# Splitting part of the mixing weights ahead of time, during the FFNs, and fetching the two parts from DRAM

## The chip, the core and the metric

The kernel runs on one core of a Trainium2 chip. The metric is the device time of one execution in microseconds. Engines are named as in the profile: PE (TensorE, matmuls), PEld (its weight loads), DVE (VectorE), ACT (ScalarE), POOL (GpSimd), SP (SyncE, which issues every DMA of this kernel, in one queue).

## What is computed

Two layers of a hybrid backbone over 256 context and 256 latent tokens of width 1024. Each layer is an FFN half step, a token mixing and a second FFN half step:

```
for l in range(2):
    x = ffn_sublayer(x, ...); s = ffn_sublayer(s, ...)          # swiglu, 1024 -> 2*2816 -> 1024
    hx, hs = modulate(rms_norm(x)), modulate(rms_norm(s))
    out_x, out_s = token_mixing(hx, hs, ...)                    # one input projection mix_w_in, then
                                                                # retention + attention + RWKV-7,
                                                                # three branch projections, gates, w_out
    x = x + gate * out_x;  x = ffn_sublayer(x, ...)
    if l == 0: s = s + gate * out_s;  s = ffn_sublayer(s, ...)
```

Everything is float32. The shift, scale and gate vectors ("ada") come from a conditioning vector times a 1024 x 9216 matrix per layer.

## The kernel before

**Dense products.** A float32 product is made of three passes on PE: both operands are split into a high part (rounded to the PE's fp32r format) and the remainder, and `mm3` (lines 185 to 188) adds high x high, high x low and low x high. Activations lie feature-major, 512 tokens as columns: 256 of the context, 256 of the latent stream. In layer 1, after the mixing's inputs, only the 256 latent columns are left.

**Weights.** All weights of a stage lie in DRAM in the order of use, in groups of four 128 x 128 blocks (128 x 512 float32, 256 KB): `w0a`, `w0b`, `w0c` are the first FFN, the mixing and the second FFN of layer 0, `w1a`, `w1b`, `w1c` those of layer 1. Each FFN has 132 groups; `w0b` is loaded in 214 and `w1b` in 211 group loads (a few groups are loaded twice). `Weights.get` brings a group in:

```
raw = s.mk([128, PB * 128], "raw", 8)[:, :cols]
hi = s.mk([128, PB * 128], "whi", 4, F32R)[:, :cols]
lo = s.mk([128, PB * 128], "wlo", 3, F32R)[:, :cols]
s.last = nc.sync.dma_start(out=raw, in_=...).ins        # L113, SP
nc.scalar.copy(hi, raw)                                  # L114, ACT
nc.vector.tensor_sub(lo, raw, hi.bitcast(F32))           # L115, DVE
```

The last argument of a tile is the number of its buffers: 8 raw tiles, 4 high parts, 3 low parts. A raw buffer comes free when DVE has made the low part of it, a `whi` or `wlo` buffer when PE has used it.

**Stages.** In time the program runs: first FFN of layer 0 (up to about 385 us), first mixing (to about 1270), second FFN of layer 0 (to about 1655), first FFN of layer 1 (to about 2047), second mixing (to about 2737), last FFN. Beside the FFNs run the ada tasks: `ada_tile` (lines 227 to 243) loads a 512 KB tile `m` on SP (L234, 3 buffers) and reduces it with two DVE instructions (L236, L237). In the first FFN some ada tiles go through PE instead (`adaT`, L254). The mixing holds the recurrences: `rw_prep`, `rw_merge`, `rw_chain` (lines 901 to 1112) are chains of small steps that go back and forth between PE, ACT, DVE, and POOL, where 31 pairs of POOL instructions (L1006, L1007) invert small triangular blocks, with DMAs through DRAM on both sides.

**Order.** The order on each engine is not the order of the code: a list scheduler with its own model of times places the instructions of all engines while the program is built, so loads of a later stage can stand ahead of work of an earlier one. On the chip every engine, and the SP queue too, then works strictly in the order that was written; an instruction that waits holds up all behind it. `tc.issue_after(mark)` keeps a DMA behind another one.

Of the kernel before, what the change touches and what calls it, by code (L numbers as in the profile page):

```python
# [7 lines left out]
F32 = mybir.dt.float32  # L8
F32R = mybir.dt.float32r
# [16 lines left out]
PB = 4  # L26
# [60 lines left out]


class Weights:
    def __init__(s, nc, mk, ap, plan, pool=False):  # L90
        s.pool = pool
        s.nc, s.mk, s.ap, s.plan = nc, mk, ap, plan
        s.n = sum(len(b) for _, b in plan)
        s.at, s.pos, s.cur = 0, 0, {}

# [8 lines left out]
    def get(s, t, n=1):  # L104
        p = t // PB
        if p not in s.cur:
            nc = s.nc
            cols = min(PB, s.n - p * PB) * 128
            raw = s.mk([128, PB * 128], "raw", 8)[:, :cols]
            hi = s.mk([128, PB * 128], "whi", 4, F32R)[:, :cols]  # L110
            lo = s.mk([128, PB * 128], "wlo", 3, F32R)[:, :cols]
            o = p * PB * 16384
            s.last = nc.sync.dma_start(out=raw, in_=s.ap[o:o + 128 * cols].rearrange("(p c) -> p c", p=128)).ins  # L113
            nc.scalar.copy(hi, raw)  # L114
            nc.vector.tensor_sub(lo, raw, hi.bitcast(F32))  # L115
            s.cur = {q: v for q, v in s.cur.items() if q == p - 1}
            s.cur[p] = (hi, lo)
        hi, lo = s.cur[p]
        c = (t % PB) * 128
        return hi[:, c:c + 128 * n], lo[:, c:c + 128 * n]  # L120


def body(nc, tc, I, O, es, dbg=None):
# [251 lines left out]
    def ffn(l, base, W, H, S, tasks, last=False, lead=True):  # L375
        c = span(S)
        gate = sm(16, "gate", 2).rearrange("p (k s) -> p k s", s=2)
        slots, done = 2 * FT + 16 - 8, [0, 0]

        def run(n):  # L380
            done[0] += n
            while done[1] < min(len(tasks), len(tasks) * done[0] // slots):
                tasks[done[1]]()
                done[1] += 1

        for hf in range(2):
            hid = []
            if hf == 0:
                os = [ps(t) for t in ("mm", "mm", "rx", "rx", "ap", "sc")[:2 * G3]]
                first(W, "first", H, [c] * len(os), os, 1 if lead and len(S) == 2 else 0)  # L390
            for j in range(HF):
                p = hf * HF + j
                if p < G3:
                    pg, pu = os[2 * p:2 * p + 2]
                else:
                    pg, pu = ps("mm"), ps("mm")
                    dense(W, f"g{p}", H, c, pg)
                    dense(W, f"u{p}", H, c, pu)
                sg = ft()
                A.activation(sg[:, c], pg[:, c], AF.Silu)  # L400
                V.tensor_tensor(sg[:, c], sg[:, c], pu[:, c], ALU.mult)  # L401
                h = pair("hid", HF)
                split(hl(h, c), sg[:, c])
                hid.append(h)
                run(2)
            if hf == 0:
                V.tensor_scalar(gate, mods[l, base + 2], 0.5, None, ALU.mult)
            for n in range(KT):
                if hf == 1 and n == KT - 1 and len(S) == 2:
                    last_out(W, f"o{hf}.{n}", hid, gate)  # L410
                    run(1)
                    continue
                po = ps("mm")
                dense(W, f"o{hf}.{n}", hid, c, po)
                residual(n, po, gate, S)
                run(1)
                if hf == 1:
                    if last:
                        SP.dma_start(out=O["out"][n], in_=xs[n][:, CS[1]])
                    else:  # L420
                        sq_acc(n, S)

    def load_x():
        for kt in range(KT):
# [797 lines left out]
    ada_cols()  # L1222
    ada_cond()
    vf = dp.tile([4, 128, 512], F32, name="vf", tag="vf")
    for l in range(2):
        S = both if l == 0 else lat

        def tasks(ll, ms, mark=None):
            return [lambda m=m, kt=kt: ada_tile(ll, m, kt, False, mark) for m in ms for kt in range(KT)]

        if l == 0:
            def fine(kt):
                ada_pe(0, 1, kt)
                ada_tile(0, 0, kt, True)
            H = norm(0, 0, 0, both, fine)
            tk = tasks(0, range(2, 9))
        else:
            H = norm(1, 0, 0, both)
            ada_cond()
            tk = tasks(1, range(5, 9))  # L1240
        W = Weights(nc, mk, I[f"w{l}a"], plan_ffn("f1i", "f1o"))
        ffn(l, 0, W, H, both, tk, lead=(l > 0))
        if not RC:
# [3 lines left out]
        xd = dp.tile([8, 128, 512], F32, name="xd", tag="xd", bufs=2)  # L1247
        for kt in range(KT):
            mark = SP.dma_start(out=xd[kt], in_=xs[kt]).ins
        W = Weights(nc, mk, I[f"w{l}b"], plan_mix(l), True)  # L1250
        ms, mark = mix(l, W, H, S, vf, mark, mst)
        mix_out(l, W, ms, S, xd)
        H = norm(l, 2, 6, S)
        tk = []
        if l == 0:
            with tc.issue_after(mark):
                ada_cond()
            tk = tasks(1, range(5), mark)
        W = Weights(nc, mk, I[f"w{l}c"], plan_ffn("f2i", "f2o"))
        ffn(l, 6, W, H, S, tk, last=(l == 1))  # L1260

# [103 lines left out]
```

## Time and profile before

| | |
|---|---|
| three runs | 2952.3, 2956.5, 2960.07 us (median 2956.5) |
| the profiled execution | 2952.92 us, of it 2951.1 us span |
| granted PE clock, mean of the span | 0.963 |
| busy: PE, PEld, DVE, ACT, POOL | 95%, 81%, 68%, 45%, 13% |
| DMA | 400.97 MB, 136 GB/s on average |

The span is the time from the first to the last instruction of the trace; 1.8 us lie outside it. Busy time says what an engine did, not what the others waited for. A busy PE is not a PE at its peak: matmuls overlap in the pipeline, and the clock granted to it may be lower than full. In the views below "waited for" rows read: engine, line and what it waits for; the time in total, how often, and the longest. SPq is SP's queue.

### The profile page before, as it was taken

Reading aid. Unit: us, or ns where it says so; the run is one execution under the profiler, and the core shown is the slowest. Engines: PE = TensorE matmul, PEld = TensorE weight load, DVE = VectorE, ACT = ScalarE, POOL = GpSimd, SP = SyncE. Lnnn points to the kernel's source line nnn. Section 1 sums busy time; section 2 is a strip of 40 time slices with the busy share of each in tenths; the row PEclk is TensorE's granted clock in tenths of the full one; section 3 lists DMA queues with packets and bytes.
Section 4 is the critical chain, followed back from the end, with each engine's and each line's share of the span. In section 5 each row is a group of like instructions: output and inputs, shape, how many; then the busy total and the mean of one; then the engine's idle time right before and its main releaser. Section 6 shows DMA issues by size and latency. Waiting matters only on the chain.

```text
span 2951.1 us, 47422 instructions
## 1 busy us (share of the span) xinstructions
PE 2796.3 (95%) x16761; PEld 2387.8 (81%) x16761; DVE 1999.8 (68%) x4677; ACT 1320.8 (45%) x2968; POOL 375.0 (13%) x1068
## 2 busy tenths in 40 slices
PE   8999999889999999899999999999989898999999
PEld 7888888677877787688888888888878787888999
DVE  7967668666685766467746567455787776577655
ACT  3322245556555654333223332223467665564544
POOL 0000000522032211000000000000033433330000
PEclk9999999889999999999999999999999999799999
DMA  7656444212332146433534435353334233146554
GB/s 268 232 188 192 155 127 132 76 49 82 115 97 78 50 128 216 154 104 126 184 136 162 145 121 173 108 174 120 123 109 112 80 114 113 53 131 202 171 179 154
DMA packets 259727, 400.97 MB, mean 136 GB/s; under 512 B 78752, under 2 KB 96288, under 8 KB 259488
## 3 DMA queue, kind: packets, MB, share of 16 engines
q1 hardware_dynamic: 259488, 397.93, 42.5%
q8 instruction: 132, 2.16, 0.3%
q14 instruction: 107, 0.88, 0.1%
HBM read 368.33 MB, written 25.82 MB: 134 GB/s over the span
## 4 chain that ended last, share of the span: by engine, by line
PE 79%; DVE 6%; POOL 5%; DMA 4%; ACT 2%; issue 2%; SPq 1%; POOLq 0%; DVEq 0%; ACTq 0%
PE ps_mm L186 20%; PE ps_mm L188 20%; PE ps_mm L187 20%; POOL cst L1007 3%; POOL cst L1006 2%; PE ps_mm L364 2%; PE ps_po L774 1%; PE ps_rf L974 1%; DVE wlo L115 1%; PE ps_rx L1084 1%; DMA z<-td 1%; PE ps_po L559 1%; PE ps_rx L1077 1%; PE ps_rx L364 1%; PE ps_rx L1105 1%
## 5 line engine op out<-in xcount | busy, mean ns | idle before, releaser
L114 ACT CAST whi<-raw 128x512 fp32r<-128x512 f32 x954 | 564.6, 617 | 698.9 <-PE ps_mm L187 362.4
L186 PE MATMUL ps_mm<-hall,whi 128*128 128x512 f32 (+1 forms) x2320 | 841.6, 363 | 5.7 <-DVE ft L693 1.5
L188 PE MATMUL ps_mm<-hall,wlo 128*128 128x512 f32 (+1 forms) x2320 | 841.1, 363 | 2.3 <-DVE wlo L115 2.2
L187 PE MATMUL ps_mm<-hall,whi 128*128 128x512 f32 (+1 forms) x2320 | 838.3, 362 | 0.0
L115 DVE TENSOR_TENSOR wlo<-raw,whi 128x512 fp32r<-128x512 f32 x954 | 645.5, 692 | 98.2 <-ACT whi L114 68.4
L186 PEld LDWEIGHTS ps_mm<-hall,whi 128*128 128x128 f32 x2320 | 440.8, 190 | 75.2 <-ACT kv L711 2.0
L188 PEld LDWEIGHTS ps_mm<-hall,wlo 128*128 128x128 f32 x2320 | 439.0, 189 | 75.9 <-DVE wlo L115 4.7
L187 PEld LDWEIGHTS ps_mm<-hall,whi 128*128 128x128 f32 x2320 | 439.7, 190 | 71.3 <-issue 0.3
L186 PE MATMUL ps_mm<-hid,whi 128*128 128x512 f32 (+1 forms) x737 | 260.7, 354 | 0.0
L187 PE MATMUL ps_mm<-hid,whi 128*128 128x512 f32 (+1 forms) x737 | 259.9, 354 | 0.0
L188 PE MATMUL ps_mm<-hid,wlo 128*128 128x512 f32 (+1 forms) x737 | 257.4, 354 | 0.0
L1006 POOL TENSOR_TENSOR cst<-acc,cst 128x60 f32<-128x60 f32 (+24 forms) x496 | 167.9, 339 | 613.7 <-DMA acc<-ad__10934 59.4
L373 DVE SCALAR_TENSOR_TENSOR x<-ps_mm,cst,x 128x256 f32<-128x256 f32 x136 | 61.0, 481 | 193.7 <-PE ps_mm L188 193.6
L401 DVE TENSOR_TENSOR ft<-ft,ps_mm 128x512 f32<-128x512 f32 (+1 forms) x80 | 49.6, 621 | 209.0 <-PE ps_mm L188 199.4
L851 POOL TENSOR_TENSOR ll<-lora,lh 128x512 fp32r<-128x512 f32 x8 | 10.5, 1316 | 1367.9 <-DMA cst<-gup 953.9
L1007 POOL TENSOR_TENSOR cst<-cst 128x60 f32<-128x60 f32 (+24 forms) x496 | 177.2, 357 | 38.0
L236 DVE SCALAR_TENSOR_TENSOR ft<-m,cd 128x1024 bf16<-128x1024 f32 x136 | 163.0, 1221 | 8.7 <-DMA m<-ada 8.7
L237 DVE SCALAR_TENSOR_TENSOR m<-m,cd 128x1024 f32<-128x1024 f32 x136 | 165.6, 1223 | 0.7
L187 PEld LDWEIGHTS ps_mm<-hid,whi 128*128 128x128 f32 x737 | 139.1, 189 | 19.5
L186 PEld LDWEIGHTS ps_mm<-hid,whi 128*128 128x128 f32 x737 | 139.0, 189 | 19.4
L188 PEld LDWEIGHTS ps_mm<-hid,wlo 128*128 128x128 f32 x737 | 138.5, 189 | 19.5
L186 PE MATMUL ps_mm<-whi,hall 128*128 128x256 f32 x416 | 120.7, 291 | 8.2 <-DVE rr_v L799 5.1
(339 smaller groups left out, 4518.7 us busy)
## 6 DMA issues: line engine op xcount, KB each, us to landing
m<-ada SPq DMA_DIRECT2D x136, 512.0 KB, 4.3
raw<-w0b SPq DMA_DIRECT2D x214, 256.0 KB, 2.9
raw<-w1b SPq DMA_DIRECT2D x211, 256.0 KB, 3.1
raw<-w0a SPq DMA_DIRECT2D x132, 256.0 KB, 2.8
raw<-w0c SPq DMA_DIRECT2D x132, 256.0 KB, 4.4
raw<-w1a SPq DMA_DIRECT2D x132, 256.0 KB, 4.3
raw<-w1c SPq DMA_DIRECT2D x132, 256.0 KB, 3.9
gd<-ft SPq DMA_DIRECT2D x24, 256.0 KB, 2.0
```

The lines of the kernel that those rows point to most:

```text
L114: nc.scalar.copy(hi, raw)
L115: nc.vector.tensor_sub(lo, raw, hi.bitcast(F32))
L186: PE.matmul(o, w[0], h[0], start=start, stop=False)
L187: PE.matmul(o, w[0], h[1], start=False, stop=False)
L188: PE.matmul(o, w[1], h[0], start=False, stop=stop)
L236: V.scalar_tensor_tensor(junk, raw, 1.0, st["cond"][0], ALU.mult, ALU.mult, accum_out=md[:, kt, 0:1])
L237: V.scalar_tensor_tensor(raw, raw, 1.0, st["cond"][1], ALU.mult, ALU.mult, accum_out=md[:, kt, 1:2])
L364: PE.matmul(o[:, p], w[k, j][q], hl(H[k], p)[0], start=(k == 0 and q == 0 and p.start == c.start), stop=False)
L373: V.scalar_tensor_tensor(xs[n][:, CS[s]], o[:, CS[s]], gate[:, n, s:s + 1], xs[n][:, CS[s]], ALU.mult, ALU.add)
L401: V.tensor_tensor(sg[:, c], sg[:, c], pu[:, c], ALU.mult)
L1006: G.tensor_tensor(w, acc[j // 16][:, j % 16, j + 1:32].unsqueeze(1).to_broadcast([128, m, n]), tt[:, 0:m, j:j + 1].to_broadcast([128, m, n ...
L1007: G.tensor_tensor(tt[:, 0:m, j + 1:32], tt[:, 0:m, j + 1:32], w, ALU.add)
```

## The change

`Weights` gets a table `apart` of groups that are already split. For 30 groups of `w0b` (every fifth up to group 145) and 93 of `w1b` (every second), `ahead` loads the raw group (L114 of the new kernel), makes the high part on ACT and the low part on POOL (not DVE), and writes both to DRAM scratch tiles `wd` (L142). The tiles come from the ring `rt`, 8 buffers, which the mixing uses otherwise. In the mixing, `group` fetches such a group as two DMAs into two `raw` buffers (L123), with no cast and no subtraction; a fetched pair stays in its two `raw` buffers until PE has used it. The tasks are blended with the ada tasks of the FFNs: those of `w0b` in the first FFN, those of `w1b` half in the second FFN of layer 0 and half in the first FFN of layer 1.

```
+    def group(s, p):
+        nc = s.nc
+        cols = min(PB, s.n - p * PB) * 128
+        if p in s.apart:
+            w = [s.mk([128, PB * 128], "raw", 8)[:, :cols] for _ in range(2)]
+            for j in range(2):
+                nc.sync.dma_start(out=w[j], in_=s.apart[p][j])
+            return [t.bitcast(F32R) for t in w]
...
+    def ahead(s, p, mk, dram, mark=None):
+        nc = s.nc
+        raw, hi, lo = mk(F32), mk(F32R), mk(F32R)
+        with mark if mark is not None else nullcontext():
+            s.load(p, raw)
+        nc.scalar.copy(hi, raw)
+        nc.gpsimd.tensor_sub(lo, raw, hi.bitcast(F32))
+        for d, t in zip(dram, (hi, lo)):
+            nc.sync.dma_start(out=d, in_=t.bitcast(F32))
+        s.apart[p] = dram
...
+    WB = [Weights(nc, mk, I[f"w{l}b"], plan_mix(l), {}) for l in range(2)]
+    far = [list(range(0, 150, 5)), list(range(0, WB[1].n // PB, 2))]
...
-            tk = tasks(0, range(2, 9))
+            tk = blend(tasks(0, range(2, 9)), aheads(0, WB[0], far[0]), 0.25)
...
-            tk = tasks(1, range(5, 9))
+            tk = blend(tasks(1, range(5, 9)), aheads(1, WB[1], far[1][len(far[1]) // 2:]))
...
-            tk = tasks(1, range(5), mark)
+            tk = blend(tasks(1, range(5), mark), aheads(1, WB[1], far[1][:len(far[1]) // 2], mark))
```

`blend` merges two lists of tasks evenly (the second one starting at the share `late` of the first).

What the scheduler made of it shows at three places. The first is SP's queue in the first FFN, about the thirteenth to the twentieth load of `w0a`. Before:

```order
L113 DMA raw<-w0a 128x512
L234 DMA m<-ada 128x1024
L254 DMA m<-adaT 128x1024
L113 DMA raw<-w0a 128x512 x2
L234 DMA m<-ada 128x1024
L254 DMA m<-adaT 128x1024
```

Now, at the same place (`rt<-w0b` is the load of a group to be split, `wd..<-rt` are the writes of its high and then its low part):

```order
L257 DMA m<-ada 128x1024
L114 DMA raw<-w0a 128x512
L114 DMA rt<-w0b 128x512
L142 DMA wd_5_917<-rt 128x512
L277 DMA m<-adaT 128x1024
L142 DMA wd_5_917<-rt 128x512
L257 DMA m<-ada 128x1024
L142 DMA wd_10_1017<-rt 128x512
L114 DMA rt<-w0b 128x512
L114 DMA raw<-w0a 128x512
L142 DMA wd_10_1017<-rt 128x512
```

All 30 groups of `w0b` are handled within the first 62 of the 132 loads of `w0a`; between the 12th and the 36th there are now 17 loads `rt<-w0b`, 34 writes and 29 ada tiles (before: 24 ada tiles and neither).

The second place is SP's queue in the second FFN of layer 0. Before, a stretch of it:

```order
L113 DMA raw<-w0c 128x512
L234 DMA m<-ada 128x1024 x2
L113 DMA raw<-w0c 128x512 x3
L234 DMA m<-ada 128x1024 x2
L113 DMA raw<-w0c 128x512
```

Now:

```order
L114 DMA rt<-w1b 128x512
L142 DMA wd_60_15272<-rt 128x512
L257 DMA m<-ada 128x1024
L114 DMA raw<-w0c 128x512
L142 DMA wd_62_15281<-rt 128x512
L114 DMA rt<-w1b 128x512
L114 DMA raw<-w0c 128x512
L142 DMA wd_62_15281<-rt 128x512
L114 DMA raw<-w0c 128x512
L142 DMA wd_64_15376<-rt 128x512
```

All 93 groups of `w1b` stand here, the first shortly ahead of the first `x<-xd` load at the end of the first mixing, the last next to the last load of `w0c`; none is left in the first FFN of layer 1. For 77 of the 93 the next `rt` load stands behind the write of the high part; for 16 ahead of it.

The third place is DVE in the second mixing, where the retention's decay tables (`dt`), the RWKV columns (`rr_k`, `rr_v`) and the attention keys (`kl`) are made. Before:

```order
L490 TENSOR_TENSOR dt<-dt,cst 128x128
L115 TENSOR_TENSOR wlo<-raw,whi 128x512
L950 TENSOR_SCALAR rtt<-rtt,cst 128x256
L799 SCALAR_TENSOR_TENSOR rr_k<-ps_mm,cst,rr_k 128x2x255
L493 TENSOR_TENSOR dt<-dt,ft 128x384
L556 TENSOR_TENSOR ft<-ps_sc,dt 128x256
L115 TENSOR_TENSOR wlo<-raw,whi 128x512
L718 TENSOR_TENSOR kl<-ps_ap,kd 64x512
L719 TENSOR_TENSOR kl<-ps_ap,kd 64x512
L798 SCALAR_TENSOR_TENSOR rr_v<-ps_mm,cst,rr_v 128x2x255
L115 TENSOR_TENSOR wlo<-raw,whi 128x512
```

Now (35 is added to the line numbers here, 15 to that of the subtraction):

```order
L528 TENSOR_TENSOR dt<-dt,ft 128x384
L985 TENSOR_SCALAR rtt<-rtt,cst 128x256
L130 TENSOR_TENSOR wlo<-raw,whi 128x512
L591 TENSOR_TENSOR ft<-ps_sc,dt 128x256
L833 SCALAR_TENSOR_TENSOR rr_k<-ps_mm,cst,rr_k 128x2x255
L834 SCALAR_TENSOR_TENSOR rr_k<-ps_mm,cst,rr_k 128x2x255
L753 TENSOR_TENSOR kl<-ps_ap,kd 64x512
L754 TENSOR_TENSOR kl<-ps_ap,kd 64x512
```

Every second `wlo` is gone. Over the program the casts `whi` on ACT and the subtractions `wlo` on DVE go from 954 to 810 each: 36 fewer in the first mixing (30 groups, some fetched twice) and 108 fewer in the second.

## Rows read from the trace of the kernel before

**Rows 1.** Busy time, share of the span and instructions of each engine.
```profile
PE 2796.3 (95%) x16761; PEld 2387.8 (81%) x16761; DVE 1999.8 (68%) x4677; ACT 1320.8 (45%) x2968; POOL 375.0 (13%) x1068
```

**Rows 2.** Stretches: length, busy PE, PEld, DVE, ACT, POOL; clock, DMA share, GB/s.
```profile
8.00:24.00 16.00, 11.03 (x52) 10.95 (x52) 10.80 (x30) 8.67 (x14) 0.00 (x0) 1.00 1.05 394
24.00:185.00 161.00, 160.59 (x732) 131.65 (x732) 147.67 (x281) 46.90 (x87) 0.00 (x0) 1.00 0.68 229
...
385.00:1233.00 848.00, 791.27 (x4941) 658.75 (x4940) 579.00 (x1558) 442.29 (x1092) 183.10 (x532) 0.95 0.35 105
1233.00:1655.00 422.00, 408.37 (x1926) 337.47 (x1925) 269.41 (x502) 131.09 (x230) 0.00 (x0) 0.98 0.45 151
1655.00:2047.00 392.00, 387.46 (x1848) 322.70 (x1847) 226.12 (x416) 116.27 (x207) 0.00 (x0) 1.00 0.39 130
2047.00:2737.00 690.00, 631.28 (x4707) 558.02 (x4706) 508.73 (x1397) 411.44 (x1035) 191.72 (x532) 0.93 0.40 118
```

**Rows 3.** Chain of waits that ended last, share of the span by engine.
```profile
PE 79%; DVE 6%; POOL 5%; DMA 4%; ACT 2%; issue 2%; SPq 1%; POOLq 0%; DVEq 0%; ACTq 0%
```

**Rows 4.** What PE waited for in the second mixing, 2047 to 2737 us: total, times, longest.
```profile
PE ps_rx L1077 <- DVE cst L1100: 7.2, 2, 6.8
PE ps_mm L186 <- DVE rr_v L799: 5.1, 2, 4.9
PE ps_rx L1077 <- DVE rb L1111: 4.7, 4, 2.3
...
PE ps_rx L1088 <- ACT ve L1086: 3.3, 3, 2.5
```

**Rows 5.** Costliest groups: the cast and the subtraction of the weights.
```profile
L114 ACT CAST whi<-raw 128x512 fp32r<-128x512 f32 x954 | 564.6, 617 | 698.9 <-PE ps_mm L187 362.4
...
L115 DVE TENSOR_TENSOR wlo<-raw,whi 128x512 fp32r<-128x512 f32 x954 | 645.5, 692 | 98.2 <-ACT whi L114 68.4
```

**Rows 6.** SP's waits in the second mixing, 2146 to 2664 us.
```profile
SPq L1010 <- POOL cst L1007: 50.6, 6, 14.8
```

**Rows 7.** DMA issues: count, KB each, median us from issue to landing.
```profile
raw<-w0a SPq DMA_DIRECT2D x132, 256.0 KB, 2.8
raw<-w0c SPq DMA_DIRECT2D x132, 256.0 KB, 4.4
...
m<-adaT SPq DMA_DIRECT2D x8, 512.0 KB, 5.6
```

**Rows 8.** SP's issues: duration ns min/median/max, first to last start us.
```profile
L113 SPq DMA_DIRECT2D raw<-w0c x132: 327/382/1367, 1267.2 to 1650.4; - x132
```
**Rows 9.** The same for the loads at the end of the mixings.
```profile
L1209 SPq DMA_DIRECT2D x<-xd x16: 326/384/432, 1233.2 to 2727.1; - x16
```

**Rows 10.** Timeline of the second FFN: start us, duration us, engine, line.
```profile
1400.20 0.40 PE L186 MATMUL ps_mm<-hall,whi 128*128 128x512 f32 x1
...
1400.90 0.40 PE L186 MATMUL ps_mm<-hall,whi 128*128 128x512 f32 x1
```

**Rows 11.** SP's waits in the second FFN, 1270 to 1655 us.
```profile
SPq L234 <- DVE m L237: 140.5, 24, 15.9
SPq L234 <- DVE ft L236: 49.0, 2, 31.4
```

**Rows 12.** Timeline of the second mixing, DVE and POOL beside each other.
```profile
2181.45 0.39 POOL L1007 TENSOR_TENSOR cst<-cst 128x72 f32<-128x72 f32 x1
2181.58 0.81 DVE L115 TENSOR_TENSOR wlo<-raw,whi 128x512 fp32r<-128x512 f32 x1
2181.92 0.64 POOL L1006 TENSOR_TENSOR cst<-acc,cst 128x68 f32<-128x68 f32 x1
...
2182.63 0.38 POOL L1007 TENSOR_TENSOR cst<-cst 128x68 f32<-128x68 f32 x1
```

**Rows 13.** The one 128x512 subtraction that POOL does before: ns min/median/max.
```profile
L851 POOL TENSOR_TENSOR ll<-lora,lh x8: 1264/1276/1539, 410.1 to 2303.9; 128x512 fp32r<-128x512 f32 x8
```

More of the change, by code (lines that the diff above doesn't have):

```diff
@@ L89, with __init__ @@
 class Weights:
-    def __init__(s, nc, mk, ap, plan, pool=False):
-        s.pool = pool
-        s.nc, s.mk, s.ap, s.plan = nc, mk, ap, plan
+    def __init__(s, nc, mk, ap, plan, apart={}):
+        s.nc, s.mk, s.ap, s.plan, s.apart = nc, mk, ap, plan, apart
         s.n = sum(len(b) for _, b in plan)
@@ L106, in get @@
         if p not in s.cur:
[L107 to L115, printed above, removed]
             s.cur = {q: v for q, v in s.cur.items() if q == p - 1}
-            s.cur[p] = (hi, lo)
+            s.cur[p] = s.group(p)
         hi, lo = s.cur[p]
@@ L120, in get, with load @@
         return hi[:, c:c + 128 * n], lo[:, c:c + 128 * n]
+    def load(s, p, raw):
+        o, cols = p * PB * 16384, raw.shape[1]
+        s.last = s.nc.sync.dma_start(out=raw, in_=s.ap[o:o + 128 * cols].rearrange("(p c) -> p c", p=128)).ins
+    def group(s, p):
[6 more added lines that the diff above has]
+            return [t.bitcast(F32R) for t in w]
+        raw = s.mk([128, PB * 128], "raw", 8)[:, :cols]
+        hi = s.mk([128, PB * 128], "whi", 4, F32R)[:, :cols]
+        lo = s.mk([128, PB * 128], "wlo", 3, F32R)[:, :cols]
+        s.load(p, raw)
+        nc.scalar.copy(hi, raw)
+        nc.vector.tensor_sub(lo, raw, hi.bitcast(F32))
+        return hi, lo
+    def ahead(s, p, mk, dram, mark=None):
+        nc = s.nc
+        raw, hi, lo = mk(F32), mk(F32R), mk(F32R)
+        with mark if mark is not None else nullcontext():
+            s.load(p, raw)
+        nc.scalar.copy(hi, raw)
+        nc.gpsimd.tensor_sub(lo, raw, hi.bitcast(F32))
+        for d, t in zip(dram, (hi, lo)):
+            nc.sync.dma_start(out=d, in_=t.bitcast(F32))
+        s.apart[p] = dram
 def body(nc, tc, I, O, es, dbg=None):
@@ L421, in ffn, with aheads, one, blend @@
                         sq_acc(n, S)
+    def aheads(l, W, ps_, mark=None):
+        def one(p):
+            t = dp.tile([2, 128, PB * 128], F32, name=f"wd{l}_{p}", tag=f"wd{l}_{p}")
+            W.ahead(p, lambda dt: mk([128, PB * 128], "rt", 8, dt), (t[0], t[1]), None if mark is None else tc.issue_after(mark))
+        return [lambda p=p: one(p) for p in ps_]
+    def blend(a, b, late=0.0):
+        n = len(a)
+        at = [((i + 0.5) / n, 0, t) for i, t in enumerate(a)] + [(late + (1 - late) * (i + 0.5) / max(len(b), 1), 1, t) for i, t in enumerate(b)]
+        return [t for _, _, t in sorted(at, key=lambda x: x[:2])]
     def load_x():
@@ L1249, in body @@
             mark = SP.dma_start(out=xd[kt], in_=xs[kt]).ins
-        W = Weights(nc, mk, I[f"w{l}b"], plan_mix(l), True)
+        W = WB[l]
         ms, mark = mix(l, W, H, S, vf, mark, mst)
```

## The prediction

> **What bounds the kernel now.** I read the busy shares first, then the stages, then the waits inside the stage that is not full. PE is busy 95% of the span [rows 1], so the first question is where the rest lies. The stretches [rows 2] answer it: in the FFNs (24 to 185, 1655 to 2047 us) PE is full or nearly so at a granted clock of 1.00, while in the first mixing (taken here as 385 to 1233) it is idle for 848 - 791.3 = 56.7 us and in the second for 690 - 631.3 = 58.7 us. There the granted clock is also lower, 0.95 and 0.93 on average, that is, part of the time at 1.2 instead of 2.4 GHz after PE had been idle; counted as lost time this is 0.05 x 848 = 42 us and 0.07 x 690 = 48 us. So about 99 us can be won at most in the first mixing and 107 us in the second. The reader should see in the chain of waits [rows 3] that PE is 79% of it and DVE, POOL, DMA and ACT share some 17%, and in PE's waits [rows 4] that in the second mixing it waits in many small pieces, for DVE and ACT. DVE is busy there for 508.7 of 690 us, 74% [rows 2]: work that PE waits for stands in DVE's queue behind weight subtractions.
>
> **What the change takes out of the mixings.** One cast costs 617 ns on ACT and one subtraction 692 ns on DVE [rows 5]. The second mixing loses 108 of each: 66.6 us of ACT, 74.7 us of DVE. The first loses 36 of each: 22.2 and 24.9 us. None of this lies on PE, so only a shorter queue can pay. My estimate takes the delay behind a busy engine to grow as its busy share over its idle share. Second mixing: DVE falls from 509 to 434 us, over the 660 us that it might then take a share of 0.66 instead of 0.74; the ratio falls from 2.8 to 1.9, by 31%, and 31% of 107 us is 33 us. First mixing: 579 to 554 of 848 us, 2.15 to 1.88, 12% of 99 us, 12 us. The bounds are 0 (every wait is the latency of a chain, not a queue) and the whole 107 and 99 us.
>
> From this goes the price of shorter prefetch. A fetched pair holds two of eight raw buffers until PE has used it; before, SP could be 8 raw and 3 low-part groups, 11 in all, ahead of PE, now about 5. A group of the second mixing lasts 690 / 211 = 3.3 us, so the lead falls from 36 to about 17 us, and SP is held there up to 14.8 us by a POOL chain [rows 6], plus a landing of some 3 us. That is just at the edge: 2 to 3 us. I enter **-30 us** for the second mixing and **-10 us** for the first.
>
> **What it adds to the FFNs.** PE gets no work. ACT gets 123 casts (76 us, of which 57 in the second FFN, where it is busy 131 of 422 us) and POOL, idle there [rows 2], 123 subtractions of 1.28 us [rows 13]: both fit beside PE. The costs are in SP's queue and in the DMA engines, since each group is loaded once more and written as two.
>
> *Second FFN of layer 0.* All 93 groups stand between the `x<-xd` loads, first issued at 1233.2 us [rows 9], and the last load of `w0c`, at 1650.4 [rows 8]: 417 us. In most cases SP issues the load of a group, must then wait at the write of its high part until the load has landed and ACT has cast it, and only then comes the next load; weight loads for PE stand behind that wait. One such cycle costs a landing, a cast of 0.62 us and an issue of about 0.38 us [rows 5, 8]. With the landing of `w0a`, 2.8 us, this is 3.8 us, with that of `w0c`, 4.4 us, 5.4 us, with the slower `adaT`, 5.6 us, 6.6 us [rows 7]. Counting the 16 overlapped cycles half, 85 cycles take 323, 459 or 561 us. SP's lead pays for the first part: three passes over four blocks at 0.70 / 3 = 0.233 us a matmul [rows 10] make 2.8 us a group, 11 groups 31 us. That the lead holds so much shows in the waits of up to 15.9 and once 31.4 us for an ada buffer [rows 11] in a stage where PE idles 13.6 us in all. So 448 us are free, and the cycle decides from 448 / 85 = 5.3 us on. I take the landing nearest in kind, `w0c`: 459 - 448 = **+10 us**; the ends are 0 and 561 - 448 = +113 us.
>
> The bytes alone fit: 93 x 0.79 MB, 132 + 16 weight groups of 0.26 MB, 40 ada tiles of 0.52 MB and the rest make about 136 MB in 448 us, 304 GB/s, against 394 GB/s that the trace shows at the start [rows 2].
>
> *First FFN.* The 30 groups are crowded into its first half, where the ada tiles are too. From the 12th to the 36th load of `w0a` SP moves 24 x 0.26 + 29 x 0.52 + 51 x 0.26 = 34.9 MB. PE takes 24 x 2.8 = 67 us for those groups; at 394 GB/s the DMA engines take 89 us [rows 2]. The 22 us that are missing come from SP's lead as far as it has been built up by then; before, this stretch moved 229 GB/s and PE was full. Bounds 0 (lead pays all) and +40 (nothing is paid, and DVE, at 147.7 of 161 us, cannot catch up its ada work). I take **+10 us**.
>
> The Trainium skill, "DMA: Bandwidth & Descriptors", section Specifications, gives about 358 GB/s as the limit of HBM for one core. The trace has 394 GB/s over 16 us, so here the measurement decides; by the page's figure the same 34.9 MB would take 97 us, the term would be some 8 us larger, and the second FFN would still fit.
>
> **The sum** against the profiled execution: 2952.9 - 30 - 10 + 10 + 10 = **2933 us**. That execution lies 3.6 us under the median of the three runs, 2956.5, inside their spread. A measurement of this kernel can tell about 0.3%, 9 us, from no change.
>
> **Rivals.**
>
> *SP's chain starves the second FFN (slower).* The mechanism is the cycle above. For it: 77 of 93 cycles have no overlap, landings grow when more is in flight (2.8 us where loads go one by one, 4.4 in bursts [rows 7]), and ACT may hold a cast behind an activation that waits for PE. Against it: SP's waits of 16 us and more there cost PE nothing before [rows 11], and few transfers are in flight while SP waits. It decides from a landing of 5.3 - 1.0 = 4.3 us on. At 5.0 us the cycle is 6.0, 85 of them 510 us, +62; with the first FFN at +20 and the mixings at -40 this gives 2952.9 + 42 = 2995 us. Chance 0.32.
>
> *The waits in the mixings are latency, not queue (same).* POOL's and the DMAs' share of the chain [rows 3] does not get shorter when DVE has less to do, and the longest of PE's waits [rows 4] are single steps of the recurrence. Then the mixings give 15 to 20 us, the FFNs cost 20, and the time stays at about 2953 us. Chance 0.11.
>
> *POOL's subtractions slow DVE in the first FFN (same).* Where a weight subtraction and POOL's work meet, DVE's takes 0.81 instead of 0.69 us and POOL's small one 0.64 instead of 0.38 [rows 5, 12]. In 24 to 185 us DVE has 161 - 147.7 = 13.3 us to spare [rows 2]. At 0.12 us for each meeting, two for each of 30 subtractions, this is 7 us and hidden. If DVE had to wait out the whole POOL instruction, it would be 30 x 1.28 = 38 us, 25 more than there is room for: 2952.9 - 20 + 25 = 2958 us. Chance 0.06. The Trainium skill, "GPSIMD Engine Reference", section Key points, says that GpSimd shares its SBUF interfaces with VectorE and contends with DVE instructions that have two SBUF inputs; by that rule every subtraction and every ada instruction meets POOL, and the trace agrees that there is a price, of 0.12 us on DVE's side. By the same rule fewer subtractions let POOL's chains in the mixings run faster, which would be part of the -30.
>
> That the change might not do what it says is excluded by the order: 144 casts and 144 subtractions are gone.
>
> **How the numbers follow.** The forecast has the chance 0.51. The range reaches from 2880 us, where both mixings give about half of what can be won (107 / 2 + 99 / 5 = 73 us) and the FFNs cost nothing, to 3000 us, where SP's chain costs 62 us or a little more; beyond lie the landing of 5.6 us, which gives some 3046 us, and mixings that give nearly all. The likeliest case has a range of its own, 2900 to 2944 us. Faster by over 0.3%: 0.51. Within 0.3%: 0.17, from the second and third rival. Slower: 0.32.
>
> **What would show it.** Right: in the profile after, the second mixing is some 30 us shorter with DVE busy about 434 us; PE stays above 95% in the first and second FFN of layer 0, DMA there near 300 GB/s; SP waits at the writes for casts, for 3 to 5 us each. Wrong: gaps of PE in the second FFN with SP standing at the writes and landings over 5 us (the first rival), PE idle as before in the mixings in spite of a DVE share of 0.65 (the second), DVE full and weight subtractions over 0.8 us in the first FFN (the third).

## The result and the profile after

The changed kernel takes 2998.9 us (median of 4 runs, 2983.1 to 3007.8) against 2954.4 (4 runs) before: the ratio is 1.0153, with an interval of 1.0129 to 1.0178. It is slower by 44 us, where 20 us less was forecast. The profiled execution took 2995.6 us, its span is 2993.8.

The stages show where. Each is taken from the last residual addition of the stage before to its own last one (L373 before, L396 after), in one profiled execution per kernel; as the weight loads run ahead of PE, such an end lies 13 to 48 us behind the times given ahead, which follow the loads. This is such a row of the changed kernel, for the first FFN; the second number of the start times is the end of the stage:

```profile
L396 DVE SCALAR_TENSOR_TENSOR x<-ps_mm,cst,x x32: 467/477/486, 206.9 to 437.0; 128x256 f32<-128x256 f32 x32
```

| us | first FFN | first mixing | second FFN, layer 0 | first FFN, layer 1 | second mixing | last FFN |
|---|---|---|---|---|---|---|
| before | 405.6 | 912.7 | 376.8 | 377.1 | 677.6 | 197.7 |
| after | 437.0 | 910.2 | 395.4 | 378.6 | 670.9 | 198.1 |
| difference | +31.4 | -2.5 | +18.6 | +1.5 | -6.7 | +0.4 |

The mixings gave 9 us where 40 were entered, the FFNs of layer 0 cost 50 where 20 were. The busy shares, which answer to [rows 1], and the costs of POOL's new subtraction, from the page of the changed kernel:

```profile
PE 2804.5 (94%) x16761; PEld 2391.5 (80%) x16761; DVE 1997.3 (67%) x4533; ACT 1306.9 (44%) x2947; POOL 535.6 (18%) x1191
...
L130 DVE TENSOR_TENSOR wlo<-raw,whi 128x512 fp32r<-128x512 f32 x810 | 591.5, 747 | 149.9 <-ACT whi L129 117.2
...
L140 POOL TENSOR_TENSOR rt<-rt 128x512 fp32r<-128x512 f32 x123 | 185.8, 1511 | 590.8 <-ACT rt L139 515.3
```

DVE has 144 subtractions less and is as busy as before (1997 against 1999.8 us): the mean of one has grown from 692 to 747 ns. POOL's takes 1511 ns, not the 1276 of [rows 13]. Both engines are slower at the same work, which is the first trace of the cause.

The stretches of the changed kernel answer to [rows 2] (length; busy PE, PEld, DVE, ACT, POOL; clock, DMA share, GB/s):

```profile
24.00:195.00 171.00, 148.82 (x659) 121.00 (x660) 160.37 (x261) 59.18 (x107) 44.93 (x26) 0.94 0.92 320
...
1272.00:1700.00 428.00, 404.36 (x1861) 330.65 (x1862) 316.67 (x474) 168.33 (x306) 126.54 (x87) 0.97 0.88 300
...
2105.00:2780.00 675.00, 619.54 (x4672) 549.54 (x4671) 437.72 (x1248) 351.70 (x921) 174.98 (x532) 0.92 0.51 158
```

In the first, PE is idle for 22.2 us where it was full before. The finer stretches show one hole, with DVE full in it and the granted clock down in the same stretch, between stretches at 1.00 and 0.98:

```profile
80.00:100.00 20.00, 18.60 (x80) 14.64 (x78) 19.21 (x27) 6.46 (x12) 7.16 (x4) 1.00 0.91 326
100.00:120.00 20.00, 4.58 (x11) 3.62 (x12) 19.93 (x30) 5.99 (x11) 7.31 (x4) 0.59 0.95 331
120.00:140.00 20.00, 20.00 (x86) 16.05 (x85) 20.00 (x32) 7.93 (x15) 4.03 (x3) 0.98 0.95 310
```

PE's waits say for what. In 24 to 240 us:

```profile
PE ps_mm L211 <- DVE wlo L130: 19.9, 2, 16.8
```

and in the second FFN, 1272 to 1700 us:

```profile
PE ps_mm L211 <- DVE wlo L130: 8.8, 10, 1.6
```

It is DVE's subtractions for the FFN's own weights that come late, not loads.

**What DVE does in that time.** The costliest groups of DVE in 24 to 240 us (busy us, mean ns, idle before), first of the kernel before, then of the changed one:

```profile
L237 DVE SCALAR_TENSOR_TENSOR m<-m,cd 128x1024 f32<-128x1024 f32 x43 | 52.2, 1223 | 0.0
L236 DVE SCALAR_TENSOR_TENSOR ft<-m,cd 128x1024 bf16<-128x1024 f32 x43 | 51.9, 1223 | 3.1 <-DMA m<-ada 3.1
L115 DVE TENSOR_TENSOR wlo<-raw,whi 128x512 fp32r<-128x512 f32 x73 | 49.2, 688 | 0.0
```

```profile
L260 DVE SCALAR_TENSOR_TENSOR m<-m,cd 128x1024 f32<-128x1024 f32 x41 | 56.9, 1393 | 0.1
L259 DVE SCALAR_TENSOR_TENSOR ft<-m,cd 128x1024 bf16<-128x1024 f32 x41 | 54.1, 1331 | 5.8 <-DMA m<-ada 5.6
L130 DVE TENSOR_TENSOR wlo<-raw,whi 128x512 fp32r<-128x512 f32 x62 | 51.2, 836 | 4.4 <-ACT whi L129 3.1 <-issue 1.3
```

The same instructions take 170, 108 and 148 ns longer in the mean, 41 x 0.170 + 41 x 0.108 + 62 x 0.148 = 20.6 us in these three groups. A mean hides that most are as before and a few take twice as long. The timeline of the changed kernel shows a meeting (start, duration):

```profile
96.19 1.22 DVE L260 SCALAR_TENSOR_TENSOR m<-m,cd 128x1024 f32<-128x1024 f32 x1
96.21 2.35 POOL L140 TENSOR_TENSOR rt<-rt 128x512 fp32r<-128x512 f32 x1 [5.27 <-DMA raw<-w0a]
...
97.33 2.31 DVE L260 SCALAR_TENSOR_TENSOR m<-m,cd 128x1024 f32<-128x1024 f32 x1
...
99.57 0.68 DVE L234 TENSOR_TENSOR hid<-ft,hid 128x512 fp32r<-128x512 f32 x1
```

POOL's subtraction, 1.26 us alone, starts just behind a DVE instruction and ends 1.1 us late; the next DVE instruction, 1.22 us alone, ends 1.1 us late in turn. From 96.19 to 99.64 us the two engines did 1.22 + 1.26 + 1.22 = 3.70 us of work in 3.45 us: one after the other, with hardly any overlap. It depends on what the DVE instruction reads. Two of the same size in the second FFN of the changed kernel (1347.3 to 1743 us; ns min/median/max):

```profile
L130 DVE TENSOR_TENSOR wlo<-raw,whi x132: 676/683/1789, 1347.6 to 1739.2; 128x512 fp32r<-128x512 f32 x132
L424 DVE TENSOR_TENSOR ft<-ft,ps_mm x20: 673/677/689, 1395.5 to 1684.3; 128x512 f32<-128x512 f32 x20
```

The first reads both tiles from SBUF, the second one of them from PSUM; the second never gets longer, although 13 of its kind in the whole trace run beside a POOL subtraction, for 6.3 us together. Over the whole trace, DVE's instructions that meet one of the 123 subtractions take 89 us more than the median of the same instruction without a meeting, 0.72 us for each subtraction. So the 99 us that 144 subtractions less should save DVE (0.69 us each) come back for the most part.

### The profile page after: what moved, and what is told of

It reads as the page before. It is cut to its first block, busy times and chain, and to the rows that moved or that the text cites. A ratio compares the mean times of both kernels' runs of the same rounds, so it can differ in the third digit from the quotient of the medians.

```text
span 2993.8 us, 48457 instructions
## 1 busy us (share of the span) xinstructions
PE 2804.5 (94%) x16761; PEld 2391.5 (80%) x16761; DVE 1997.3 (67%) x4533; ACT 1306.9 (44%) x2947; POOL 535.6 (18%) x1191
## 5 line engine op out<-in xcount | busy, mean ns | idle before, releaser
L211 PE MATMUL ps_mm<-hall,wlo 128*128 128x512 f32 (+1 forms) x1962 | 724.5, 370 | 25.5 <-DVE wlo L130 25.5
L209 PE MATMUL ps_mm<-hall,whi 128*128 128x512 f32 (+1 forms) x1962 | 722.3, 368 | 5.9 <-DVE ft L613 3.3
L210 PE MATMUL ps_mm<-hall,whi 128*128 128x512 f32 (+1 forms) x1962 | 721.9, 368 | 0.0
L130 DVE TENSOR_TENSOR wlo<-raw,whi 128x512 fp32r<-128x512 f32 x810 | 591.5, 747 | 149.9 <-ACT whi L129 117.2
L129 ACT CAST whi<-raw 128x512 fp32r<-128x512 f32 x810 | 482.6, 618 | 360.2 <-PE ps_mm L210 172.4
L211 PEld LDWEIGHTS ps_mm<-hall,wlo 128*128 128x128 f32 x1962 | 372.2, 190 | 93.2 <-DVE wlo L130 31.2
L209 PEld LDWEIGHTS ps_mm<-hall,whi 128*128 128x128 f32 x1962 | 373.6, 190 | 70.5 <-DVE ft L613 3.7
L210 PEld LDWEIGHTS ps_mm<-hall,whi 128*128 128x128 f32 x1962 | 372.8, 190 | 64.6 <-issue 0.2
L140 POOL TENSOR_TENSOR rt<-rt 128x512 fp32r<-128x512 f32 x123 | 185.8, 1511 | 590.8 <-ACT rt L139 515.3
L139 ACT CAST rt<-rt 128x512 fp32r<-128x512 f32 x123 | 76.5, 622 | 304.7 <-DMA rt<-w1b 204.3
L260 DVE SCALAR_TENSOR_TENSOR m<-m,cd 128x1024 f32<-128x1024 f32 x136 | 177.1, 1305 | 0.8
L1042 POOL TENSOR_TENSOR cst<-cst 128x60 f32<-128x60 f32 (+24 forms) x496 | 164.1, 331 | 38.2
L396 DVE SCALAR_TENSOR_TENSOR x<-ps_mm,cst,x 128x256 f32<-128x256 f32 x136 | 60.8, 479 | 138.6 <-PE ps_mm L211 138.5
```

The costliest lines, as they stand in the source:

```text
L140: nc.gpsimd.tensor_sub(lo, raw, hi.bitcast(F32))
L209: PE.matmul(o, w[0], h[0], start=start, stop=False)
L210: PE.matmul(o, w[0], h[1], start=False, stop=False)
L211: PE.matmul(o, w[1], h[0], start=False, stop=stop)
L260: V.scalar_tensor_tensor(raw, raw, 1.0, st["cond"][1], ALU.mult, ALU.mult, accum_out=md[:, kt, 1:2])
L396: V.scalar_tensor_tensor(xs[n][:, CS[s]], o[:, CS[s]], gate[:, n, s:s + 1], xs[n][:, CS[s]], ALU.mult, ALU.add)
```

## The experiments

Each kernel was run 4 to 10 times, against the kernel before on the same chip, whose medians lay between 2952.9 and 2954.1 us. A "without" says what the edit takes from the changed kernel. The stages are those of one profiled execution each; it lies 13 us under the median for m3_all_ready, 9 us under it for a8_held_late and b1_paced_held, and within some 5 us of it for the others:

| us | total (median) | ratio | first FFN | first mixing | second FFN, layer 0 | first FFN, layer 1 | second mixing |
|---|---|---|---|---|---|---|---|
| a2_no_writes | 3001.6 | 1.0154 | 437.3 | 910.0 | 395.7 | 377.3 | 681.8 |
| a1_no_pool_sub | 2958.5 | 1.0016 | 427.1 | 899.7 | 380.8 | 378.8 | 668.3 |
| a4_second_only | 2987.5 | 1.0133 | 405.1 | 916.2 | 399.6 | 378.5 | 682.3 |
| m1_fetch_two | 2935.6 | 0.9944 | 406.5 | 897.0 | 377.2 | 378.3 | 674.7 |
| m2_fetch_one | 2919.6 | 0.9872 | 406.6 | 896.1 | 376.8 | 378.6 | 661.4 |
| m3_all_ready | 2913.1 | 0.9866 | 406.7 | 884.7 | 376.8 | 378.1 | 651.3 |
| a6_held | 2995.0 | 1.0136 | 421.5 | 906.4 | 393.6 | 384.8 | 684.3 |
| a8_held_late | 2972.3 | 1.0060 | 423.2 | 894.2 | 388.6 | 383.2 | 671.5 |
| b2_paced_no_pool | 2938.2 | 0.9968 | 412.3 | 896.2 | 382.0 | 377.7 | 670.4 |
| b1_paced_held | 2963.4 | 1.0041 | 410.7 | 897.4 | 385.3 | 387.9 | 670.2 |
| b3_paced_held_dve | 2943.3 | 0.9970 | 406.2 | 896.7 | 383.2 | 387.2 | 666.5 |
| b5_dve_second | 2963.8 | 1.0043 | 405.4 | 916.7 | 380.3 | 384.5 | 679.1 |

### Which part of the splitting ahead costs the FFNs

**Without POOL's subtraction** (the writes, casts and loads stay):

```
-        raw, hi, lo = mk(F32), mk(F32R), mk(F32R)
+        raw, hi = mk(F32), mk(F32R)
...
-        nc.gpsimd.tensor_sub(lo, raw, hi.bitcast(F32))
-        for d, t in zip(dram, (hi, lo)):
+        for d, t in zip(dram, (hi, hi)):
```

> The low part is not computed: the high part is written twice, so POOL has no subtraction, while loads, casts, writes and fetches are as in the change. Stages are told by the last residual addition of each (first FFN 405.6 us before, 437.0 with the change; second FFN of layer 0 lasts 376.8 before, 395.4 with the change). Theory 1, POOL's subtractions hold up DVE: no DVE instruction of the ada tiles lasts over 1.3 us (with the change up to 2.3), the first FFN ends at 415 to 420 us, the second FFN lasts 377 to 385, the whole about 2965 to 2975 us. Rival 2, SP's chain and the DMA engines: nothing changes, 437 and 395, about 2999 us. Rival 3, the order on DVE (a run of seven ada tiles with no weight subtraction between): the gap of PE near 100 us stays, the first FFN ends at 430 or later, while the second FFN may gain.

**Without the writes** (the subtraction stays):

```
-        for d, t in zip(dram, (hi, lo)):
-            nc.sync.dma_start(out=d, in_=t.bitcast(F32))
-        s.apart[p] = dram
```

> Loads, casts and POOL's subtractions stay, but nothing is written to DRAM and the mixings split their weights as before. So POOL meets DVE as in the change, while SP waits for no cast and the DMA engines move 63 MB less. Theory 1 (POOL holds up DVE): weight subtractions and ada instructions in the first FFN are again up to 1.1 us longer, the first FFN ends at 415 us or later and the second FFN lasts 385 or more. Rival 2 (SP's waits and the DMA engines): both FFNs are back at 405.6 and 376.8 us. Total 2965 to 2995 under theory 1, 2950 to 2956 under rival 2.

**Only the groups of the second mixing** (`far[0]` empty):

```
-    far = [list(range(0, 150, 5)), list(range(0, WB[1].n // PB, 2))]
+    far = [[], list(range(0, WB[1].n // PB, 2))]
```

> Only the 93 groups of the second mixing, none of the first. If the stages add up: the first FFN is back at 405 us, the first mixing 912, the second FFN of layer 0 some 395, the second mixing 671: 2999 - 31 + 2 = about 2969 us. If the second FFN's loss were a consequence of the first one's: 377 there, about 2950 us.

The writes cost nothing that can be seen: without them 3001.6 us and the same FFNs, though SP waits for no cast and the second FFN moves 199 instead of 300 GB/s. Without the subtraction 40 of the 44 us are gone (2958.5 us, where 2965 to 2975 were expected); the second FFN is at +4.0 us against before, although SP still stands at the writes for casts (102.8 us in 1272 to 1700 us). In the profiled executions 9.9 us of this lie in the first FFN, 14.6 in the second and 10.5 in the first mixing. The first FFN, 427.1 us, is not back at the 415 to 420 us that were expected. PE in 24 to 240 us of that kernel, and the DVE group of the ada tiles there, back at its 1221 ns:

```profile
PE ps_mm L210 <- DVE wlo L130: 13.1, 1, 13.1
```

```profile
L259 DVE SCALAR_TENSOR_TENSOR m<-m,cd 128x1024 f32<-128x1024 f32 x41 | 50.0, 1221 | 0.2
```

So the first FFN has a second cause: it is still 21.5 us longer than before, with no POOL in it. DVE's timeline of the same kernel shows the hole, from one weight subtraction to the next:

```profile
87.25 0.69 DVE L130 TENSOR_TENSOR wlo<-raw,whi 128x512 fp32r<-128x512 f32 x1
87.86 1.22 DVE L259 SCALAR_TENSOR_TENSOR m<-m,cd 128x1024 f32<-128x1024 f32 x1
89.62 1.23 DVE L258 SCALAR_TENSOR_TENSOR ft<-m,cd 128x1024 bf16<-128x1024 f32 x1 [0.53 <-DMA m<-ada]
91.56 1.23 DVE L258 SCALAR_TENSOR_TENSOR ft<-m,cd 128x1024 bf16<-128x1024 f32 x1 [0.71 <-DMA m<-ada]
...
108.31 1.22 DVE L259 SCALAR_TENSOR_TENSOR m<-m,cd 128x1024 f32<-128x1024 f32 x1
109.45 0.69 DVE L130 TENSOR_TENSOR wlo<-raw,whi 128x512 fp32r<-128x512 f32 x1
```

For 22.2 us DVE makes no low part; fourteen ada instructions, of seven tiles, stand there with only small ones of other kinds between, and DVE even waits for some of their loads with the weight's subtraction queued behind. The code says why: `blend` puts both lists into one, and the FFN runs that list evenly by its length. With `late` = 0.25 the first quarter of the ada tiles comes alone, so they run ahead of the pace that they had when they were the whole list, in the stretch where DVE was already 92% busy [rows 2]. At DVE's 24th weight subtraction 21 ada tiles are done, and 16 before the change.

The run with the second mixing's groups alone keeps the second FFN's loss (399.6 us) with a first FFN as before: it is no consequence of the first one's. Its total, 2987.5 us, is 18 us above the 2969 that were expected from adding the stages; in the profiled execution the second mixing alone, 682.3 us, is 11 over and gains nothing.

### What the relief is worth in the mixings

In these three nothing is split during the FFNs; one group, split once, stands in for all. With the change's two fetches:

```
+    aheads(0, WB[0], [0])[0]()
+    for l in range(2):
+        WB[l].apart.update({p: WB[0].apart[0] for p in far[l]})
...
-            tk = blend(tasks(0, range(2, 9)), aheads(0, WB[0], far[0]), 0.25)
+            tk = tasks(0, range(2, 9))
```

(and so for the other two blends);

> The mixing's side of the change alone: the same groups are fetched as two parts, but all from one pair of tiles that was split once at the start, so the FFNs have no extra work (the product with those groups is of other weights). Queue theory (a shorter DVE queue is worth 30 and 10 us): second mixing, from the last residual of one FFN to the last of the mixing, 677.6 us before, now below 650, total below 2925 us. Latency theory: second mixing 665 to 678 us, first mixing within 10 us of 912.7, total 2938 to 2955 us.

with one fetch that serves as both parts, which takes one raw buffer instead of two:

```
-            w = [s.mk([128, PB * 128], "raw", 8)[:, :cols] for _ in range(2)]
-            for j in range(2):
-                nc.sync.dma_start(out=w[j], in_=s.apart[p][j])
-            return [t.bitcast(F32R) for t in w]
+            w = s.mk([128, PB * 128], "raw", 8)[:, :cols]
+            nc.sync.dma_start(out=w, in_=s.apart[p][0])
+            return [w.bitcast(F32R)] * 2
```

> As the mixing's side alone, but one fetch and one raw buffer instead of two serve as high and low part (the product with those groups is of other weights). It tells what the second fetch and the shorter prefetch cost. If the lead is what eats the gain (m1_fetch_two: first mixing 897, second 675, total 2936 us): 10 us or more better, 2925 or less. If not: within 5 us of it, 2931 to 2941.

and with that for all groups of both mixings (`far = [list(range(WB[l].n // PB)) for l in range(2)]`):

> All groups of both mixings are taken as ready: one fetch of a tile split once, used as high and low part, no cast and no weight subtraction in the mixings (the products are of other weights). This is the most that DVE and ACT relief could ever give. Queue theory: both mixings lose most of the idle time and clock, some 80 us each, total 2790 to 2830 us. Latency theory: each mixing gives at most 25 us, total 2900 us or more.

The relief itself is worth 2954 - 2935.6 = 18 us, nearly all of it in the first mixing (-15.7, -2.9 in the second). The second fetch and the shorter lead together take 16.1 us (2935.6 against 2919.6); in the profiled executions 13.3 us lie in the second mixing, where every second group is a pair. The run does not tell the two apart. With no cast and no subtraction left in either mixing, 41 us are won. The second mixing of the last run, and what PE still waits for there:

```profile
2047.00:2698.00 651.00, 601.36 (x4664) 531.27 (x4664) 373.04 (x1142) 296.49 (x826) 160.86 (x532) 0.96 0.43 124
```

```profile
PE ps_rx L1166 <- DVE rb L1163: 7.0, 2, 4.8
PE ps_po L593 <- DVE ft L590: 5.5, 5, 2.4
```

DVE is at 57%, and PE is idle for 49.6 us, against 58.7 before with DVE at 74%. The waits are for single steps of the chains, as in [rows 4].

### The pace, and where the subtraction is done

**Held** and **held and later**: the load of an ahead group goes out only behind the latest weight load of the FFN; in the second run the first mixing's groups also start at half of the list.

```
-            W.ahead(p, lambda dt: ..., (t[0], t[1]), None if mark is None else tc.issue_after(mark))
+            W.ahead(p, lambda dt: ..., (t[0], t[1]), tc.issue_after(W_now[0].last))
...
-            tk = blend(tasks(0, range(2, 9)), aheads(0, WB[0], far[0]), 0.25)
+            tk = blend(tasks(0, range(2, 9)), aheads(0, WB[0], far[0]), 0.5)
```

> The change with each early load held on SP's queue behind the FFN weight load that precedes it in the code, so that the 30 groups spread over the last three quarters of the first FFN and the 93 over both the second FFN of layer 0 and the first of layer 1 (47 and 46). POOL's subtractions stay, all 123. Crowding theory (POOL's subtractions and the ada tiles do harm only where DVE has no room): the first FFN ends at 405 to 412 us (437.0 with the change), the second FFN lasts 377 to 385 (395.4), the first FFN of layer 1 377 to 385 (378.6), the mixings together 5 to 20 us less than before, total 2940 to 2960 us. Rival, every subtraction of POOL costs PE time wherever it stands: 30 x 1.1 us in the first FFN and 93 x 0.2 in the others, 2990 us or more.

> As the held version, and the early loads of the first FFN start at half of it instead of at a quarter, when the ada tiles are sparser. Crowding theory: the first FFN ends at 405 to 408 us, some 0 to 5 us earlier than with the start at a quarter; total 2938 to 2955 us. Rival, each subtraction costs wherever it stands: no difference to the held version.

Neither mends the first FFN (421.5 and 423.2 us, where 405 to 412 and 405 to 408 were expected): both keep the merged list, and DVE still does eleven ada instructions, of five to six tiles, between two weight subtractions (84.0 to 101.4 us in the held run), with 21 ada tiles done at the 24th. Holding alone brings 3.8 us of the median, the later start 22.8 more. Of the 29.9 us between the two profiled executions 12 are in the first and 13 in the second mixing, whose builds differ among themselves by about as much. The 2995.0 us of the held run are where its rival, a price for every subtraction wherever it stands, put it; but the paced version below keeps all 123 subtractions and takes 2963.4.

**Paced**: every ada task keeps its former place and an ahead task hangs on the nearest one.

```
+        n, m = len(a), max(len(b), 1)
+        at = [min(int((late + (1 - late) * (i + 0.5) / m) * n), n - 1) for i in range(len(b))]
+        def both_(k):
+            a[k]()
+            for i, t in enumerate(b):
+                if at[i] == k:
+                    t()
+        return [lambda k=k: both_(k) for k in range(n)]
```

First without POOL's subtraction, not held:

> Leaves out: POOL's subtraction (the high part is written twice), and the ada tasks keep the pace they had before the change; an ahead task hangs on the ada task next to it. The run without the subtraction still had a first FFN of 427 us against 405.6. Theory (the merged list is paced by its index, and as the first part of it holds ada tasks alone, they run ahead of their pace, seven ada tiles in a row on DVE): the first FFN goes to 406 to 412 us, second FFN about 380, mixings as in the run without the subtraction (900 and 668), 2935 to 2945 us in all. Rival (the loads, writes and casts themselves take SP or the DMA engines from PE's weights in the first FFN): the first FFN stays at 420 us or more, total 2953 us or more.

The hole is gone (17 ada tiles are done at the 24th weight subtraction), and the steps add up. The median goes from 2998.9 (the change) by 40 us to 2958.5 (without POOL's subtraction), by 20 to 2938.2 (paced as well), 14.8 of them in the first FFN; the run in which the FFNs do nothing ahead has 2935.6, 18 us under the kernel before. So the 44 us are 40 for POOL's subtraction, 20 for the pace and 2.5 for all loads, casts, writes and SP's waits of 123 groups, less 18 of relief. The 2.5 us are less than the runs can tell, and they are a sum: in the profiled executions the two FFNs of layer 0 are 5.8 and 4.8 us longer here than with nothing done ahead, and the second mixing 4.3 us shorter. PE in the stretch of the hole, at 360 GB/s, with the DMA engines full:

```profile
24.00:185.00 161.00, 158.56 (x702) 128.96 (x703) 140.44 (x267) 62.65 (x114) 0.00 (x0) 0.97 0.99 360
```

The first FFN, 412.3 us, is a little above what was expected and 6.7 us longer than before, about what 2.4 us of idle time and a clock of 0.97 cost in this stretch (0.03 x 161 = 5 us). Up to 6.7 us may be the price of the full DMA engines; that it is theirs is not shown.

Then paced and held, with the subtraction on POOL, and the same with it on DVE:

> Complete kernel: ada tasks at their former pace, and the load of an ahead group held behind the latest weight load of the FFN, subtraction on POOL as in the change. Theory (POOL's subtraction holds up DVE for about its own length wherever DVE reads two tiles of SBUF): the pace gives back some 15 to 20 us of the first FFN and the subtraction keeps its price, about 10 us there (30 of 1.3 us minus DVE's slack of 13, plus a little) and 12 to 19 us in the FFNs where the groups of w1b stand: first FFN 412 to 420 us, total 2955 to 2980 us. Rival (the crowding was all of it, the subtraction is cheap once it is not crowded): first FFN 406 to 410, second 377 to 382, total 2935 to 2945 us.

```
-        nc.gpsimd.tensor_sub(lo, raw, hi.bitcast(F32))
+        nc.vector.tensor_sub(lo, raw, hi.bitcast(F32))
```

> Complete kernel: as the paced and held one, but the subtraction of the ahead groups is on DVE instead of POOL, so that it takes 0.69 us of DVE and holds up nothing. Theory (POOL's 1.3 us block DVE for nearly that long, DVE's own 0.69 us cost only that): in the first FFN 30 x 0.69 = 21 us against 13 us of slack, 8 us or less lost, in the second FFN 93 x 0.69 = 64 us against some 150 us of slack, nothing lost: first FFN 408 to 416 us, second 377 to 381, total 2935 to 2955 us, under the paced one with POOL by 10 us or more. Rival (DVE's time is what counts, whoever does it): no better than the paced one with POOL.

With POOL the first FFN, 410.7 us, is a little under what was expected, so the pace, with the hold, was the larger part of the loss there. On DVE the kernel takes 2943.3 us, ratio 0.9970 (0.9956 to 0.9985): faster than both kernels, by 9.6 and 56 us, and by 20 us than with POOL (2963.4; the two profiled executions are 11.8 us apart). More work on the busier engine is the cheaper way here. The FFNs with the groups of `w1b` have little part in this: they lose 8.5 and 10.8 us with POOL, and with DVE still 6.4 and 10.1 (383.2 and 387.2 us), where nothing was expected to be lost. So most of those 19 us, which had been expected as POOL's price, are not POOL's; their cause is not settled. In the first FFN the stretch of the former hole is full:

```profile
24.00:185.00 161.00, 161.00 (x733) 132.09 (x733) 149.69 (x283) 53.87 (x98) 0.00 (x0) 1.00 0.81 277
```

**Only the second mixing's groups**, in this form:

> Complete kernel: as the one with DVE's subtraction, but only the groups of the second mixing are split ahead, so that the first FFN has nothing added. Theory (the first FFN has no room on DVE, the later ones have): first FFN 405.5 to 407, second FFN and first FFN of layer 1 together at most 4 us longer than before, first mixing as before (913), second mixing 668 to 675 instead of 677.6: total 2944 to 2955 us. Rival (split ahead pays more in the first mixing than it costs): slower than the one with both mixings' groups by 5 us or more.

A miss: 2963.8 us instead of 2944 to 2955, 20 more than with both mixings' groups and slower than before (1.0025 to 1.0062). The two FFNs with the groups of `w1b` are 3.5 and 7.4 us longer, the first mixing, where nothing is relieved, 4 longer, and the second gains nothing (679.1). The rival is right: the gain of the best version lies mostly in the 30 groups of the first mixing (916.7 against 896.7 us). The second mixing, with the same groups in both, took 679.1 and 666.5 us; over all builds with this relief and two fetches it took 666.5 to 684.3, so that single stages are not told apart to better than some 10 us. A kernel with those alone was not run.

## Why the prediction was wrong

**Both fit beside PE** is the step that failed. It costed POOL's 123 subtractions at nothing because POOL is idle in the FFNs and PE gets no work. But they are paid on DVE, whose instructions they lengthen by 89 us: without them the kernel is 40 us faster. PE did not lose to POOL directly; it lost since DVE's low parts came late. The other terms that failed are smaller: the pace of the ada tiles, 20 us, is in no term, the relief gave 18 us instead of 40, and the loads, casts and writes cost 2.5 us instead of 20. From the forecast of -20 us this is +40 + 20 + 22 - 17.5 = 64.5 us, and the measured +44.5 is that far off.

**The price of a meeting** was in the rows and was read by half. [Rows 12] show DVE's subtraction 0.12 us longer. The 0.38 us that I set beside POOL's 0.64 are of another line, L1007; L1006 with 68 columns takes 0.31 us where no DVE instruction runs beside it (at 655.3 and 929.4 us of that trace). So POOL lost 0.33 us, more than the instruction's own length and almost three times DVE's share, which the reading left out. I took DVE's 0.12 us as a price per meeting, from an instruction of 68 columns, for one of 512. At 2 x 0.12 us for each of 30, 7 us were expected and called hidden; the 26 POOL subtractions that stand in 24 to 195 us, and at most 3 behind them, lengthened DVE's three costliest groups by 20.6 us, 0.7 to 0.8 us each. The Trainium skill, "GPSIMD Engine Reference", section Key points, says that GpSimd and VectorE contend where a DVE instruction has two SBUF inputs. The trace agrees, with 0.72 us on DVE's side for each of the 123 subtractions.

**The third rival** named the mechanism, even with the right bound (DVE waits out the whole instruction, 38 us), but only for the first FFN, and at 2958 us. In the second FFN, where DVE has 150 us to spare, I did not consider it. There the mean of DVE's weight subtraction rose to 948 ns (688 before), in the groups of 1272 to 1700 us:

```profile
L130 DVE TENSOR_TENSOR wlo<-raw,whi 128x512 fp32r<-128x512 f32 x140 | 131.0, 948 | 41.0 <-ACT whi L129 36.4 <-issue 4.5
```

Spare time in the sum doesn't help the one instruction that PE needs next, at most 3 `wlo` buffers ahead.

**First FFN, +10**: measured +31.4 in the profiled execution. My term was DMA time; what runs show is POOL (9.9 us, 437.0 against 427.1), the pace of the ada tiles (14.8, 427.1 against 412.3) and 6.7 us for the rest, with the DMA engines full. DVE had been named, but only in the upper bound. That `blend` shifts the ada tiles could be read from the code and the order.

**Second FFN, +10**: +18.6 and from another cause. SP's cycle, which was to decide from a landing of 4.3 us on, did not: the landing of `w0c` was 4.7 us, and without the subtraction the second FFN lost 4.0 us. SP's wait at the writes, in 1272 to 1700 us of the changed kernel:

```profile
SPq L142 <- ACT rt L139: 147.9, 80, 3.6
SPq L142 <- POOL rt L140: 34.7, 48, 2.0
```

That is 1.8 us each, not a landing and a cast of 4.4 + 0.62 = 5 us: between a load and its write stand other loads, which I had read in the order but not subtracted. The first rival is thereby wrong; that its sign and almost its time (2995 us) came true is luck.

**Second mixing, -30**: -6.7, and -2.9 in the run with the relief alone. DVE fell as worked out (437.7 us, forecast 434), PE's idle time only from 58.7 to 55.5 us. The formula of busy over idle share would give 56 us for the run with all weights ready (0.57 / 0.43 = 1.3 in place of 2.8, 52% of 107); it gave 26, and 49.6 of PE's 58.7 us of idle time stayed. So most of that idle time does not hang on the weights' casts and subtractions, and the second rival, which gave the mixings 15 to 20 us, was right in this (18 measured); that the rest is latency alone is not shown. The shorter lead, entered at 2 to 3 us, cost some 13 together with the second fetch.

**First mixing, -10**: the relief gave 15.7 us, more than entered. In the changed kernel only 2.5 remained. In its tail 19 of POOL's subtractions for the second mixing already stand (from 1262 us on). From the last `ps_rx` matmul to the end of the stage the changed kernel takes 77.1 us, 17 of the 19 among them; the kernel before takes 69.3, the run without the subtraction 69.2 and the two held ones, with none there, 67.8 and 68.4. So 8 of the 13 us lie where the subtractions are. With 16 of them the run of the second mixing's groups alone takes 72.0 us, with 23 the one without the writes 69.6, so the number alone does not set the price. The other 5 us are within what builds differ by.

The range, to 3000 us, held the time by a hair, for the sake of a rival whose mechanism did not happen; the likeliest case, 2900 to 2944 us, did not.

## What to carry to other kernels

An idle GpSimd is no free place for elementwise work on SBUF while VectorE is on PE's path: charge up to its whole duration to VectorE (here 0.72 us in the mean, of 1.28), and compare that with the time VectorE itself would need (0.69 us). When tasks are merged into a list that is run by its index, look at what happens to the pace of those that were there before. And before relieving a queue, run the kernel with all of its load gone: here that would have shown 41 us as the most there was to win with every group split, 18 with the groups of this change.

## What was not expected of the hardware

A 128x512 subtraction on POOL and an instruction of DVE with two inputs from SBUF run one after the other: 1.22 us became 2.31, 1.26 us became 2.35, and 3.70 us of work took 3.45 us. A DVE instruction of the same size with one input from PSUM stayed at 673 to 689 ns beside it. The DMA engines at 0.99 of their time and 360 GB/s over 161 us cost the first FFN no more than 6.7 us. PE's granted clock went down with the one hole of 16.8 us, 0.59 on average over the 20 us around it, and was at 0.98 in the next 20.
